# Cosine-similarity attention on one core: TensorE and ScalarE no longer wait on semaphores that they raise themselves

## Chip, core and metric

The kernel runs on one NeuronCore of a Trainium2 chip. The metric is device time in microseconds (us) for one execution; medians of several runs are given. "Slow" here means more than 1.5% above the fastest run of the same kernel. Ratios are the mean time of one kernel's fast runs over that of the other's of the same rounds, so they are not quite the ratio of the medians quoted beside them. "Span" is the time between the first and last instruction of the profiled execution; it is 1.7 to 2.0 us shorter than the device time. The experiments ran in three sets of rounds, on two chips; each set has its own runs of the kernel before (medians 240.59, 240.71 and 241.14 us), so kernels of different sets are best compared by their ratios.

## The reference

```python
def setup_inputs():
    batch, heads, seq, dim = 8, 12, 512, 64
    return {"Q": np.random.randn(batch, heads, seq, dim).astype(np.float32),   # K and V alike
            ..., "tau": 0.1}

def reference(Q, K, V, tau):
    Q_norm = Q / (np.linalg.norm(Q, axis=-1, keepdims=True) + 1e-10)
    K_norm = K / (np.linalg.norm(K, axis=-1, keepdims=True) + 1e-10)
    scores = np.einsum('bhqd,bhkd->bhqk', Q_norm, K_norm) / tau
    weights = np.exp(scores - np.max(scores, axis=-1, keepdims=True))
    weights = weights / (np.sum(weights, axis=-1, keepdims=True) + 1e-10)
    return np.einsum('bhqk,bhkd->bhqd', weights, V).astype(np.float32)
```

There are 96 heads. The kernel treats them as 48 pairs of heads.

## The kernel before

The kernel describes its work as a list of operations with an engine, a modelled cost and a list of the operations that each one needs. A small scheduler in the kernel puts the operations into one order per engine, and a writer then emits the instructions of each engine with semaphore waits. A semaphore is a counter: an operation can raise it when it has ended, and an engine can wait until it has reached a value. This is the writer's part that matters:

```python
    def run(self):
        nc = self.nc
        order = self.schedule()
        dma_sems, dma_count, last_out = {}, {}, {}
        for e, ops in order.items():
            for o in ops:
                for n in o.needs:
                    self.ops[n].used = True          # somebody waits for n: it must raise its semaphore
        # ... each used operation gets the next count of its engine's semaphore (o.sem, o.val)

        def write(engine, name):
            seen = {}
            for o in order[name]:
                want = {}
                for n in o.needs:
                    p = self.ops[n]
                    k = id(p.sem)
                    if p.val > max(seen.get(k, 0), want.get(k, (None, 0))[1]):
                        want[k] = (p.sem, p.val)
                for k, (sem, val) in want.items():
                    engine.wait_ge(sem, val)
                    seen[k] = val
                inst = o.emit(engine, o.bank) if o.bank else o.emit(engine)
                if o.sem is not None:
                    inst.then_inc(o.sem, o.inc)
```

For each pair `s`, TensorE does square sums (SSQ, 16 matmuls of 64 columns), transposes (TR, 8), scores (SCO, four chunks of two matmuls with 512 columns, one a head, each on half of the rows of the array) and the product of weights and V (PV, eight groups of four matmuls with 65 columns). ScalarE does one exp a chunk. VectorE divides by the row sums (RCP, NRM), and GpSimd (POOL in profiles) does most of the squaring before the square sums and part of the scaling. Matmuls write to PSUM, a memory in banks; the results of PV and of the square sums share two banks, and a bank comes free when VectorE has read it. Scores have two buffers, so the scores of chunk c need the exp of chunk c-2.

```python
            P.add(("SCO", s, c), "pe", 0.44, T0 + c - 3,
                  [("EVA", s), ("EXP", s, c - 2) if c >= 2 else key("EXP", s - 1, c + 2)], sco)
            P.add(("EXP", s, c), "act", 0.925, T0 + c,
                  [("SCO", s, c), key("PV", s - R_ET, 1, NT - 1)], lambda e, c=c, b=b: e.activation(...))
# ... [cut]
        for h in range(2):
            for t in range(NT):
                def pv(e, bank, h=h, t=t):
                    for c in range(NT):
                        last = e.matmul(
                            out=o_ps[bank][:, 65 * t : 65 * t + 65],
                            lhsT=et[iet][:, c, h, 128 * t : 128 * t + 128], rhs=vb[:, iq, c, h, :],
                            start=(c == 0), stop=(c == NT - 1))
                    return last

                op = P.add(("PV", s, h, t), "pe", 0.127, T0 + 4 + 2 * h + 0.4 * t,
                           [("EXP", s, NT - 1), ("VC", s)] + ([("PV", s, h, t - 1)] if t else []), pv,
                           take=("pv", s, h) if t == 0 else None)
# ... [cut: RCP needs the last of these groups]
            P.add(("NRM", s, h), "dve", 0.43, T0 + 5.6 + 2 * h, [("RCP", s, h), key("ST", s - R_O)],
                  lambda e, bank, h=h: e.tensor_tensor(out=ob[io][:, h], ...), give=("pv", s, h))
```

`("PV", s, h, t - 1)` is a need of one TensorE operation on another one. It keeps the four groups of a head in order for the scheduler, but the writer also turns it into a real wait.

## Time and profile before

| | before |
|---|---|
| device time, median of the first 3 runs | 241.84 us |
| span of the profiled run | 239.6 us |
| first exp starts, last exp ends, end of the span | 14.25, 232.8, 239.6 us |
| exps | 192, one every (232.8 - 14.25) / 192 = 1.138 us (the 1.133 of the prediction leaves out the length of the last exp) |

The page of the profile, part 1 (busy time of each engine, share of the span, instructions) and part 4 (the chain of work that ended last, by engine and by line):

```profile
PE 211.3 (88%) x3072; PEld 130.1 (54%) x3072; DVE 151.1 (63%) x481; ACT 192.6 (80%) x195; POOL 162.0 (68%) x148
...
PE 85%; issue 4%; ACT 3%; DVE 3%; DMA 2%; SPq 1%
PE ops L359 41%; PE scps L336 25%; PE ops L270 10%; PE tps L321 9%; ACT et L345 3%; DMA qk<-in_K_dram 2%; DVE qt L328 1%; SPq L252 1%; DVE sq L266 1%; DVE nps L288 0%; DVE nps L289 0%; DVE qn L315 0%; DVE ob L376 0%; DVE ys L293 0%; DVE nps L293 0%
```

TensorE (PE) is the chain: 85% of the span. "issue" is time in which an engine waited for nothing that the profile shows. TensorE's busy share alone would not say that it is the limit, because matmuls overlap: eight of about 197 ns take 0.42 us below. L359 is the PV matmul, L336 the scores, L345 the exp.

Part 5 of the page, three groups (line, engine, operation, output<-inputs, shapes, count | busy us, mean ns | idle time before, and what ended most of it):

```profile
L345 ACT ACTIVATE et<-scps 128x1024 bf16<-128x1024 f32 x192 | 189.2, 1023 | 32.7 <-PE scps L336 29.7
L359 PE MATMUL ops<-vb,et 128*128 128x65 bf16 x1536 | 108.3, 197 | 12.7 <-ACT et L345 1.1
...
L359 PEld LDWEIGHTS ops<-vb,et 128*128 128x128 bf16 x1536 | 67.1, 98 | 65.6 <-PE ops L359 47.8
```

ScalarE (ACT) stood idle for 29.7 us until scores came. The weight loads of PV (PEld) stood idle for 47.8 us until *other PV matmuls* ended; by an estimate from the idle times shown further below, about 34 us of this (191 x 0.18) stood directly behind a PV group.

What one such wait costs is seen in the chain of waits between 151.5 and 154.7 us (start, length, what, number of matmuls):

```profile
152.00 0.32 PE scps L336 x2
152.33 0.24 PE ops L359 x4
152.57 0.05 issue
152.62 0.31 PE ops L359 x4
152.93 0.05 issue
152.97 0.42 PE ops L359 x8
```

The group that starts at 152.62 waited for the group before it: 0.31 us, and 0.05 us until the next can start. The last line holds two groups, of which the second belongs to the next head and waits for no PV group: the two take 0.42 us, so the second adds only about 0.12 us.

The timeline of the weight loads shows the two kinds of idle time in front of PV (start, length, engine, line, operation, count, idle time before it):

```profile
147.70 0.17 PEld L359 LDWEIGHTS ops<-vb,et 128*128 128x128 bf16 x4 [0.23 <-PE tps L321]
148.06 0.17 PEld L359 LDWEIGHTS ops<-vb,et 128*128 128x128 bf16 x4 [0.18 <-PE ops L359]
148.41 0.30 PEld L359 LDWEIGHTS ops<-vb,et 128*128 128x128 bf16 x8 [0.18 <-PE ops L359]
...
150.58 0.23 PEld L321 LDWEIGHTS tps<-ident,qn 128*128 128x128 bf16 x4 [0.23 <-issue]
```

A group behind a PV group idles 0.18 us. A group behind scores idles 0.23 us, but so does a transpose behind scores (150.58), which waits for nothing on TensorE. A wait behind scores should therefore cost little.

### The profile page before, as it was taken

Reading aid. Unit: us, or ns where it says so; the run is one execution under the profiler, and the core shown is the slowest. Engines: PE = TensorE matmul, PEld = TensorE weight load, DVE = VectorE, ACT = ScalarE, POOL = GpSimd, SP = SyncE. Lnnn points to the kernel's source line nnn. Section 1 sums busy time; section 2 is a strip of 40 time slices with the busy share of each in tenths; the row PEclk is TensorE's granted clock in tenths of the full one; section 3 lists DMA queues with packets and bytes.
Section 4 is the critical chain, followed back from the end, with each engine's and each line's share of the span. In section 5 each row is a group of like instructions: output and inputs, shape, how many; then the busy total and the mean of one; then the engine's idle time right before and its main releaser. Section 6 shows DMA issues by size and latency. Waiting matters only on the chain.

```text
span 239.6 us, 7296 instructions
## 1 busy us (share of the span) xinstructions
PE 211.3 (88%) x3072; PEld 130.1 (54%) x3072; DVE 151.1 (63%) x481; ACT 192.6 (80%) x195; POOL 162.0 (68%) x148
## 2 busy tenths in 40 slices
PE   0489999889999999999999999999999999998773
PEld 0346556455655565565565565665665665654332
DVE  0667677465877767668657667667667767774322
ACT  3158998878798787898898898898898898887860
POOL 2399997929679868979939939949969935030000
PEclk9999999999999999999999999999999999999965
DMA  5999969695768569589695696699494412121121
GB/s 181 356 349 350 326 210 317 205 327 199 222 220 267 179 198 326 183 240 331 216 306 201 205 311 208 175 294 331 121 347 153 135 47 88 51 84 47 44 89 45
DMA packets 52256, 50.80 MB, mean 212 GB/s; under 512 B 3072, under 2 KB 52224, under 8 KB 52224
## 3 DMA queue, kind: packets, MB, share of 16 engines
q1 hardware_dynamic: 52224, 50.34, 65.6%
q8 instruction: 24, 0.39, 0.6%
q14 instruction: 8, 0.07, 0.1%
HBM read 37.75 MB, written 12.58 MB: 210 GB/s over the span
## 4 chain that ended last, share of the span: by engine, by line
PE 85%; issue 4%; ACT 3%; DVE 3%; DMA 2%; SPq 1%
PE ops L359 41%; PE scps L336 25%; PE ops L270 10%; PE tps L321 9%; ACT et L345 3%; DMA qk<-in_K_dram 2%; DVE qt L328 1%; SPq L252 1%; DVE sq L266 1%; DVE nps L288 0%; DVE nps L289 0%; DVE qn L315 0%; DVE ob L376 0%; DVE ys L293 0%; DVE nps L293 0%
## 5 line engine op out<-in xcount | busy, mean ns | idle before, releaser
L345 ACT ACTIVATE et<-scps 128x1024 bf16<-128x1024 f32 x192 | 189.2, 1023 | 32.7 <-PE scps L336 29.7
L359 PE MATMUL ops<-vb,et 128*128 128x65 bf16 x1536 | 108.3, 197 | 12.7 <-ACT et L345 1.1
L359 PEld LDWEIGHTS ops<-vb,et 128*128 128x128 bf16 x1536 | 67.1, 98 | 65.6 <-PE ops L359 47.8
L266 POOL TENSOR_TENSOR sq<-qk 128x1024 bf16<-128x1024 f32 x45 | 84.4, 1894 | 0.0
L315 POOL TENSOR_TENSOR qn<-qk,rk 128x512 bf16<-128x512 f32 x48 | 49.3, 1042 | 45.0 <-DVE rk L293 26.9
L336 PE MATMUL scps<-qt 64*128 64x512 bf16 x384 | 74.9, 392 | 3.0 <-ACT et L345 2.1
L373 DVE RECIPROCAL rd<-ops 128x4 f32<-128x4 f32 x96 | 17.3, 180 | 45.1 <-PE ops L359 44.8
L376 DVE TENSOR_TENSOR ob<-ops,rd 128x256 f32<-128x256 f32 x96 | 40.2, 422 | 2.6
L270 PE MATMUL ops<-sq,ident 128*128 128x64 bf16 x768 | 32.2, 197 | 8.9 <-ACT sq L263 6.4
L328 DVE COPY qt<-tps 128x1024 bf16<-128x1024 bf16 x48 | 33.0, 688 | 9.2 <-PE tps L321 8.6
L321 PE MATMUL tps<-ident,qn 128*128 128x128 bf16 x384 | 36.3, 224 | 0.5 <-DVE qt L328 0.5
L270 PEld LDWEIGHTS ops<-sq,ident 128*128 128x128 bf16 x768 | 27.7, 100 | 13.2 <-ACT sq L263 6.5
L351 POOL TENSOR_SCALAR vb<-vf 128x512 bf16<-128x512 f32 x48 | 29.6, 633 | 6.4 <-DMA vf<-in_V_dram 6.4
L315 DVE TENSOR_TENSOR qn<-qk,nps 128x512 bf16<-128x512 f32 x48 | 32.2, 670 | 0.0
L321 PEld LDWEIGHTS tps<-ident,qn 128*128 128x128 bf16 x384 | 22.9, 99 | 10.2 <-issue 5.6
L336 PEld LDWEIGHTS scps<-qt 64*128 64x128 bf16 x384 | 17.9, 93 | 17.1 <-ACT et L345 4.3
L280 DVE TENSOR_REDUCE nps<-ops 128x16 f32<-128x64 f32 x48 | 10.9, 227 | 17.2 <-PE ops L270 16.9
L288 DVE TENSOR_TENSOR nps<-nps,ys 128x32 f32<-128x32 f32 (+2 forms) x36 | 7.6, 210 | 1.2
L289 DVE SCALAR_TENSOR_TENSOR nps<-nps,ys 128x32 f32<-128x32 f32 (+2 forms) x36 | 7.5, 210 | 1.2
L263 ACT ACTIVATE sq<-qk 128x1024 bf16<-128x1024 f32 x2 | 2.1, 1056 | 6.7 <-DMA qk<-in_K_dram 6.7
L266 DVE TENSOR_TENSOR sq<-qk 128x1024 bf16<-128x1024 f32 x1 | 1.2, 1225 | 7.6 <-DMA qk<-in_K_dram 7.6
L297 DVE TENSOR_SCALAR ys<-nps 128x32 int32<-128x32 int32 (+2 forms) x18 | 3.6, 202 | 0.6
(11 smaller groups left out, 12.9 us busy)
## 6 DMA issues: line engine op xcount, KB each, us to landing
qk<-in_Q_dram SPq DMA_DIRECT2D x48, 256.0 KB, 4.5
qk<-in_K_dram SPq DMA_DIRECT2D x48, 256.0 KB, 5.4
vf<-in_V_dram SPq DMA_DIRECT2D x48, 256.0 KB, 4.7
out_dram<-ob SPq DMA_DIRECT2D x48, 256.0 KB, 4.5
```

What stands on the lines that cost most here:

```text
L266: lambda e: e.tensor_tensor(out=sqf, in0=data, in1=data, op=ALU.mult))
L270: last = e.matmul(out=o_ps[bank][:, 320:384], lhsT=ident[:, :], rhs=sq[iqs][:, :, 4 * k : 4 * k + 4], start=(k == 0), stop=(k == 15))
L280: lambda e, bank: e.tensor_reduce(out=x2[:, :, c8 : c8 + 8], in_=o_ps[bank][:, 320:384].rearrange("p (w g e) -> p w g e", w=2, e=4), axis= ...
L315: lambda e, w=w, r=r: e.tensor_tensor(out=qn[iqn][:, w].rearrange("p t h d -> p h t d"), in0=qk[iq][:, w].rearrange("p h (t d) -> p h t d" ...
L321: last = e.transpose(t_ps[:, w, t, :], qn[iqn][:, w, t].rearrange("p h d -> p (h d)"), ident[:, :])
L328: lambda e: e.tensor_copy(out=qt[iqt][:, :, :, :].rearrange("p w t x -> p (w t x)"), in_=t_ps[:, :, :, :].rearrange("p w t x -> p (w t x)")))
L336: last = e.matmul(out=sc_ps[:, 2 * b + h, :], lhsT=qt[iqt][64 * h : 64 * h + 64, 1, c, :], rhs=qt[iqt][64 * h : 64 * h + 64, 0, :, :], sta ...
L345: lambda e, c=c, b=b: e.activation(out=et[iet][:, c, :, :], in_=sc_ps[:, 2 * b : 2 * b + 2, :], func=ACT.Exp, scale=inv_tau))
L351: lambda e: e.tensor_scalar(out=vb[:, iq, :, :, 0:DIM].rearrange("p c h d -> p h c d"), in0=vf[iv][:, :, :].rearrange("p h (c d) -> p h c ...
L359: last = e.matmul(out=o_ps[bank][:, 65 * t : 65 * t + 65], lhsT=et[iet][:, c, h, 128 * t : 128 * t + 128], rhs=vb[:, iq, c, h, :], start=( ...
L373: lambda e, bank, h=h: e.reciprocal(out=rd[io][:, h, :], in_=grid(bank)[:, :, DIM]))
L376: lambda e, bank, h=h: e.tensor_tensor(out=ob[io][:, h], in0=grid(bank)[:, :, 0:DIM], in1=rd[io][:, h, :].unsqueeze(2).to_broadcast([128, ...
```

## The change

The intent is to take away waits of an in-order engine on its own semaphore. The scheduler still sees the needs; only the writer drops them, for TensorE ("pe") and ScalarE ("act").

```diff
@@ -110,8 +110,11 @@
         for e, ops in order.items():
             for o in ops:
-                for n in o.needs:
-                    self.ops[n].used = True
+                o.waits = [self.ops[n] for n in o.needs]
+                if e in ("pe", "act"):
+                    o.waits = [p for p in o.waits if p.eng != e]
+                for p in o.waits:
+                    p.used = True
@@ -131,8 +134,7 @@
             for o in order[name]:
                 want = {}
-                for n in o.needs:
-                    p = self.ops[n]
+                for p in o.waits:
                     k = id(p.sem)
```

The built programs differ only in this: 288 waits of TensorE on its own semaphore are gone (and the increments nobody reads any more). The order of instructions is the same on all five engines, and no ScalarE operation needs another one, so ScalarE's program does not change at all. Of the 288 waits, 191 stand directly behind another PV group and 97 behind other matmuls.

## The prediction

> **What bounds the kernel now.** TensorE. The chain of waits puts 85% of the span on TensorE matmuls, 41% on the P·V line alone, and about 96% in a steady stretch from 145.9 to 163.7 us (four pairs of heads, 4.44 us a pair). ScalarE is busy 192.6 us (80%), and the groups view puts 29.7 us of its idle time down to the score matmuls. Back-to-back exps follow each other every 0.924 us in the timeline (six in 5.64 us), so its 192 exps need at least 177 us.
>
> **What the change does.** It moves nothing: the order of instructions is the same on all five engines. It drops 288 waits, all on TensorE and all of one kind: the first matmul of a P·V group (4 matmuls, 65 columns) waiting for the last matmul of the previous group. ScalarE has no wait on itself, so nothing changes there. Correctness does not need these waits: the groups write different columns, and the Trainium skill (PSUM page "PSUM — Partial Sum Buffer", "Engine vs sequencer instructions") says matmuls start and complete in program order.
>
> **What one such wait costs.** In the chain of waits, a group that waits on its predecessor takes 0.30 us plus 0.05 us "issue"; a second group without the wait adds only 0.12 us (8 matmuls in 0.42 us). So 0.235 us each. The weight-load row shows the same: 0.18 us idle before the load. The skill ("TensorE: Matmul & The Clock Gate", "Step-by-step") says weight loads are pulled ahead of running matmuls; the wait forbids this between groups, and the trace agrees. Only 191 of the 288 waits follow directly on a P·V group. The other 97 follow score, transpose or square-sum matmuls; after scores, transposes without any wait on TensorE show the same 0.23 us of idle, so those waits are nearly free. Estimate: 191 x 0.235 = 45 us of TensorE time removed.
>
> **How much is on the path.** All of it until ScalarE takes over. In the steady stretch 14 waits fall in 17.77 us; without them TensorE needs 14.5 us (3.62 a pair), ScalarE 16 x 0.924 = 14.8 us (3.70 a pair). Only two score buffers couple the two, and TensorE's work between score pairs is uneven (0.55 to 1.14 us): counting the larger of it and 0.924 each time gives 15.8 us (0.987 an exp). GpSimd (3.56 us a pair) and VectorE (some 3.4 in the stretch with groups of two pairs) are close behind, so I expect 0.96 to 1.02 us an exp, against 1.133 now.
>
> Span: 14.25 us until the first exp (unchanged) + 192 x 0.98 = 188 + tail 5.4 us (6.8 less six waits of about 0.23 at the end, where the clock is low) = 207.8; plus 2.2 us between span and time: **210 us, 203 to 219**. Faster by over 2%: 0.97; within 2%: 0.025; slower: 0.005.
>
> **What would show it.** Weight loads' wait on P·V matmuls falls from 47.8 us to under 15. Sixteen P·V matmuls take about 0.6 us in the timeline, not 1.13. ScalarE's share goes from 80% to about 92%, its wait on scores from 29.7 us to under 15. The chain of waits has ScalarE as a large part (over 30%), TensorE well under 85%. First exp still at about 14.2 us. Score matmuls wait for ScalarE more than now (4.3 us). VectorE and GpSimd keep their busy times.
>
> **What would make it wrong.** GpSimd or VectorE becomes the limit in the first 100 us (GpSimd runs there without a break from 10.7 to 39.6 us): over 215. Groups after the change still do not overlap (a limit of weight load, not of the wait): 230 or more. ScalarE runs nearly without gaps: 201 to 203.

## The result, and the profile after

| | before | after |
|---|---|---|
| device time, median | 241.78 us (4 runs) | 206.24 us (4 runs: 205.14 to 207.87) |
| ratio of fast runs | 1 | 0.8537 (95%: 0.8461 to 0.8613) |
| span of the profiled run | 239.6 us | 205.6 us |
| until the first exp | 14.25 us | 14.16 us |
| first exp to end of the last | 218.6 us, 1.138 an exp | 186.8 us, 0.973 an exp |
| behind the last exp | 6.8 us | 4.6 us |

The span fell by 34.0 us: 0.1 at the head, 31.8 while exps run, 2.2 at the tail. The profiled run is one of the slower two of four (207.31 us). The mean clock granted to TensorE was 0.980 of full speed before and 0.984 after, so the clock explains little of the gain (only part of that at the tail, see below).

The same parts 1 and 4 of the page, after:

```profile
PE 182.0 (89%) x3072; PEld 120.3 (59%) x3072; DVE 146.6 (71%) x481; ACT 182.0 (89%) x195; POOL 161.8 (79%) x148
...
PE 56%; ACT 23%; DMA 11%; DVE 6%; SPq 1%; issue 1%; ACTq 0%; DVEq 0%
ACT et L347 22%; PE scps L338 20%; PE ops L361 18%; PE ops L272 10%; PE tps L323 8%; DMA out_dram<-ob 8%; DMA qk<-in_K_dram 3%; DVE qt L330 2%; DVE ob L378 2%; SPq L254 1%; ACT sq L265 1%; ACTq L151 0%; DVE nps L290 0%; DVE nps L282 0%; DVE rd L375 0%
```

And the same three groups of part 5, after:

```profile
L347 ACT ACTIVATE et<-scps 128x1024 bf16<-128x1024 f32 x192 | 178.6, 1058 | 11.5 <-PE scps L338 10.8
...
L361 PE MATMUL ops<-vb,et 128*128 128x65 bf16 x1536 | 75.0, 196 | 6.4 <-DVE ob L378 4.9
...
L361 PEld LDWEIGHTS ops<-vb,et 128*128 128x128 bf16 x1536 | 56.9, 98 | 36.7 <-issue 23.3
```

PV (now L361) fell from 41% of the chain to 18%, and from 108.3 to 75.0 us of busy time with the same 1536 matmuls of the same mean length (197 and 196 ns): they overlap now. No PV weight load waits for a PV matmul any more. The 23.3 us that are now called "issue" are the 0.23 us behind scores, which before were put down to the PV wait that ended at about the same time. The chain of waits after the change, between 135.6 and 137.5 us, reads:

```profile
135.68 0.32 PE scps L338 x2
136.00 0.66 PE ops L361 x16
136.66 0.32 PE scps L338 x2
136.99 0.48 PE ops L361 x12
```

Twelve matmuls behind scores take 0.48 us. Before, three such groups took 0.24 + 0.05 + 0.31 + 0.05 + 0.30 = 0.95 us (153.72 to 154.66 us). Two blocking waits cost 0.47 us, 0.235 each.

ScalarE's timeline after shows two regimes (idle time before each piece in brackets):

```profile
57.50 4.69 ACT L347 ACTIVATE et<-scps 128x1024 bf16<-128x1024 f32 x5 [0.68 <-PE scps L338]
64.40 15.24 ACT L347 ACTIVATE et<-scps 128x1024 bf16<-128x1024 f32 x16 [2.21 <-PE scps L338]
...
87.06 1.02 ACT L347 ACTIVATE et<-scps 128x1024 bf16<-128x1024 f32 x1 [1.69 <-PE scps L338]
88.59 1.02 ACT L347 ACTIVATE et<-scps 128x1024 bf16<-128x1024 f32 x1 [0.51 <-PE scps L338]
90.03 110.94 ACT L347 ACTIVATE et<-scps 128x1024 bf16<-128x1024 f32 x120 [0.41 <-PE scps L338]
```

From 90.03 us on, 120 exps run in 110.94 us, 0.924 each: the spacing that unhindered exps had before the change (six in 5.64 us). ScalarE is then the limit. Earlier there are gaps that the old kernel did not have in this form. The two largest after the first exp (2.21 us before 64.40 and 1.69 us before 87.06) come from VectorE, which waits for an output store. The first of them is shown here (first its line in the timeline of VectorE, then the chain of waits over the same stretch, both after the change):

```profile
63.25 0.42 DVE L378 TENSOR_TENSOR ob<-ops,rd 128x256 f32<-128x256 f32 x1 [2.80 <-DMA out_dram<-ob]
```

```profile
56.41 0.47 DVE qt L330
56.88 0.00 issue
56.88 6.28 DMA out_dram<-ob
...
63.25 0.44 DVE ob L378
63.69 0.05 issue
63.74 0.30 PE ops L361 x4
64.03 0.34 PE scps L338 x2
64.38 0.02 issue
64.40 1.94 ACT et L347 x2
```

A store issued at 56.88 us lands 6.28 us later. The normalization that wants its buffer waits for it, PV waits for the PSUM bank that the normalization holds, the scores queue behind PV, and ScalarE runs dry. This wait is new: before, no VectorE instruction waited for a store.

### The profile page after: what moved, and what is told of

It reads as the page before. It is cut to its first block, busy times and chain, and to the rows that moved or that the text cites. A ratio compares the mean times of both kernels' runs of the same rounds, so it can differ in the third digit from the quotient of the medians.

```text
span 205.6 us, 7296 instructions
## 1 busy us (share of the span) xinstructions
PE 182.0 (89%) x3072; PEld 120.3 (59%) x3072; DVE 146.6 (71%) x481; ACT 182.0 (89%) x195; POOL 161.8 (79%) x148
## 4 chain that ended last, share of the span: by engine, by line
PE 56%; ACT 23%; DMA 11%; DVE 6%; SPq 1%; issue 1%; ACTq 0%; DVEq 0%
ACT et L347 22%; PE scps L338 20%; PE ops L361 18%; PE ops L272 10%; PE tps L323 8%; DMA out_dram<-ob 8%; DMA qk<-in_K_dram 3%; DVE qt L330 2%; DVE ob L378 2%; SPq L254 1%; ACT sq L265 1%; ACTq L151 0%; DVE nps L290 0%; DVE nps L282 0%; DVE rd L375 0%
## 5 line engine op out<-in xcount | busy, mean ns | idle before, releaser
L347 ACT ACTIVATE et<-scps 128x1024 bf16<-128x1024 f32 x192 | 178.6, 1058 | 11.5 <-PE scps L338 10.8
L361 PE MATMUL ops<-vb,et 128*128 128x65 bf16 x1536 | 75.0, 196 | 6.4 <-DVE ob L378 4.9
L338 PE MATMUL scps<-qt 64*128 64x512 bf16 x384 | 75.8, 394 | 4.5 <-ACT et L347 2.8
L361 PEld LDWEIGHTS ops<-vb,et 128*128 128x128 bf16 x1536 | 56.9, 98 | 36.7 <-issue 23.3
L338 PEld LDWEIGHTS scps<-qt 64*128 64x128 bf16 x384 | 18.4, 93 | 21.6 <-ACT et L347 5.0
```

Source lines behind the costliest of these rows:

```text
L338: last = e.matmul(out=sc_ps[:, 2 * b + h, :], lhsT=qt[iqt][64 * h : 64 * h + 64, 1, c, :], rhs=qt[iqt][64 * h : 64 * h + 64, 0, :, :], sta ...
L347: lambda e, c=c, b=b: e.activation(out=et[iet][:, c, :, :], in_=sc_ps[:, 2 * b : 2 * b + 2, :], func=ACT.Exp, scale=inv_tau))
L361: last = e.matmul(out=o_ps[bank][:, 65 * t : 65 * t + 65], lhsT=et[iet][:, c, h, 128 * t : 128 * t + 128], rhs=vb[:, iq, c, h, :], start=( ...
```

## The experiments

The theory (A): a wait on TensorE's own semaphore costs the rest of the round trip of the matmul that it names, about 0.235 us where that is the matmul just issued, and nothing where it is old. TensorE was the limit, so the time fell by nearly all of it until ScalarE took over. Rivals: it is the increments (B), each wait costs the same (C), or the wait instruction has a fixed handling cost (D). All experiments leave the order of instructions on every engine as it was; only the last two pairs of kernels leave instructions out or add some.

### Increments kept, waits gone

```diff
-                for p in o.waits:
-                    p.used = True
+                for n in o.needs:
+                    self.ops[n].used = True
```

Expected: 

> The changed kernel, but every P.V group still raises the TensorE semaphore (288 increments that nobody reads). Theory A, the waits cost: 206 us, as the changed kernel. Rival B, the increments cost and the waits are free: near 241 us. If increments carry a part, between 209 and 235 us.

Measured: 206.56 us (before, in the same rounds: 240.59), ratio 0.8575, correct. Rival B falls: 288 increments that nobody waits for cost nothing that shows.

### Only the 97 waits behind other matmuls kept, and only the 191 behind PV kept

```diff
+            prev = None
             for o in ops:
                 o.waits = [self.ops[n] for n in o.needs]
-                if e in ("pe", "act"):
+                if e == "pe" and not (prev is not None and prev.key[0] != "PV"):   # == "PV" in the mirror image
                     o.waits = [p for p in o.waits if p.eng != e]
+                prev = o
```

Expected of the 97: 

> Only the 97 waits stay whose group does not follow directly on another P.V group (it follows scores, transposes or square sums). Theory A (a wait costs only what is left of the predecessor's completion when TensorE gets to it): 206 to 208 us, as the changed kernel. Rival C (every wait on the own semaphore costs the same, 35.6 us / 288 = 0.124 us each): 206 + 97 x 0.124 = 218 us.

Expected of the 191: 

> The mirror image: the 191 waits that follow directly on a P.V group stay, the other 97 go. Theory A: 240 to 242 us, as the kernel before. Rival C (all waits equal): 241.8 - 97 x 0.124 = 230 us.

Measured: 206.47 us with the 97 waits (ratio 0.8582) and 240.94 us with the 191 (ratio 1.0009). All of the gain hangs on the 191 waits that follow directly on a PV group. Rival C falls.

### The wait moved to an older group

```diff
+        groups = []
         for e, ops in order.items():
             for o in ops:
                 o.waits = [self.ops[n] for n in o.needs]
-                if e in ("pe", "act"):
+                if e == "pe":
+                    mine = any(p.eng == e for p in o.waits)
                     o.waits = [p for p in o.waits if p.eng != e]
+                    if o.key[0] == "PV":
+                        groups.append(o)
+                        if mine and len(groups) > 2:          # 8 in the second kernel
+                            o.waits.append(groups[-1 - 2])
```

Expected of two back: 

> As many waits as before on TensorE's own semaphore (285 of 288), but each waits for the P.V group two before it instead of the one before it. Theory A (what costs is the round trip of the group just issued, 0.355 us, against 0.12 us of work a group): in a run of four groups only one of three waits still blocks, for 0.355 - 0.24 = 0.115 us, so some 7 us of TensorE time come back in place of 45, and much of that hides: 206 to 211 us. Rival D (a wait on the own semaphore costs some 0.2 us of handling whatever it waits for): near 241 us.

Expected of eight back: 

> As many waits as before on TensorE's own semaphore, each for the P.V group eight before it, which has always long ended. Theory A: as the changed kernel, 206 us. Rival D (the wait instruction itself costs): 218 to 241 us.

Measured: 207.61 us two back (before 240.59; ratio 0.8601; one of four runs, 209.89, counted as slow and is not in the ratio) and 205.99 us eight back (before 240.71; ratio 0.8535; one run, 208.04, counted as slow). The built kernels have 287 and 282 waits on the own semaphore (the 285 of the expectation was a slip). So 282 such waits are free when they name a group that has ended. Rival D falls. The chain of waits of the kernel with two back shows the dose:

```profile
133.16 0.32 PE scps L344 x2
133.48 0.71 PE ops L367 x16
134.19 0.32 PE scps L344 x2
134.51 0.58 PE ops L367 x12
```

Sixteen matmuls behind scores take 0.71 us instead of 0.59 to 0.66, twelve 0.58 instead of 0.48. The expected remainder was 0.355 - 0.24 = 0.115 us for one blocking wait.

### Half of the waits gone

```diff
-                if e in ("pe", "act"):
+                if e == "pe" and o.key[0] == "PV" and o.key[2] == 0:     # the first head of each pair only
```

Expected: 

> The waits of the first head of each pair go (144, of which 84 follow directly on a P.V group), those of the second stay (144, 107 direct). Theory A, TensorE stays the limit all through at this dose: 241.8 - 84 x 0.235 = 222 us. A rival in which ScalarE or the store waits already limit after half: 210 to 216 us. A rival in which the second half of the waits is what counts (nothing until all are gone): above 232 us.

Measured: 221.04 us (before 240.71; ratio 0.9185). That is 19.7 us for 84 direct waits, 0.234 us each. At this dose every removed wait counts in full, so TensorE was the limit throughout. All 191 at this price are 45 us; the whole change brought 35.5. The second half of the waits is worth less because another limit comes in between.

### Eight output buffers, after and before

```diff
     R_QK, R_V, R_SQ, R_QN, R_QT, R_ET, R_O, R_X = 18, 6, 6, 3, 3, 3, 4, 3
+    R_OB = 8
-    ob = [sb(f"ob{i}", [128, 2, NT, DIM], f32) for i in range(R_O)]
+    ob = [sb(f"ob{i}", [128, 2, NT, DIM], f32) for i in range(R_OB)]
         # ob[io] and the store's semaphore become those of s % R_OB; and, after scheduling:
+        for o in self.list:
+            if o.key[0] == "NRM":
+                late = ("ST", o.key[1] - 8)
+                o.needs = [n for n in o.needs if n[0] != "ST"] + ([late] if late in self.ops else [])
```

Expected of the changed kernel with eight: 

> The changed kernel with eight output buffers instead of four, the order of instructions on every engine unchanged; only the normalization's wait for the store of four pairs earlier moves to the store of eight pairs earlier. Theory E (the ScalarE gaps at 57 to 65 and 79 to 90 us come from normalization waiting for a store): VectorE's wait on stores falls from 6.2 us to 0, ScalarE's wait on scores from 10.8 us to about 5, time 198 to 202 us. Rival F (another limit stands right behind, GpSimd or transfers): the waits on stores go, ScalarE's wait on scores stays at 9 us or more, time 204 to 207 us.

Expected of the kernel before with eight: 

> The kernel before, all 288 waits in place, with the same eight output buffers. Theory E says no store held it up at its slower pace, so 241 to 242 us, unchanged. If output buffers were a limit of their own: 236 us or less.

Measured: 201.10 us (200.89 to 201.60) with the change, ratio 0.8359; 241.09 us without it, ratio 1.0024. ScalarE's timeline of the faster one:

```profile
56.49 19.84 ACT L352 ACTIVATE et<-scps 128x1024 bf16<-128x1024 f32 x21 [0.68 <-PE scps L343]
76.83 2.85 ACT L352 ACTIVATE et<-scps 128x1024 bf16<-128x1024 f32 x3 [0.50 <-PE scps L343]
80.12 114.32 ACT L352 ACTIVATE et<-scps 128x1024 bf16<-128x1024 f32 x124 [0.44 <-PE scps L343]
```

VectorE no longer waits for a store, and ScalarE's wait for scores fell from 10.8 to 6.2 us, of which 3.38 are in front of the first exp. The same buffers do nothing for the slower kernel. So stores were a limit that the change itself brought to light, worth 4 to 5 us (5.1 between the medians, 4.3 by the ratios 0.8537 and 0.8359). Runs also agree better: 0.7 us apart in place of 2.7. This version beats both kernels.

### TensorE work taken away (a wrong result)

```diff
-            for k in range(16):
+            for k in range(0, 16, 2):
                 last = e.matmul(
                     out=o_ps[bank][:, 320:384], lhsT=ident[:, :], rhs=sq[iqs][:, :, 4 * k : 4 * k + 4],
-                    start=(k == 0), stop=(k == 15))
+                    start=(k == 0), stop=(k == 14))
```

Expected of the kernel before: 

> The kernel before with half of the square-sum matmuls left out (8 of 16 a pair; a wrong result on purpose), nothing else changed. A matmul there takes 0.47 us / 16 = 0.029 us, so 48 x 8 x 0.029 = 11 us of TensorE work go. Theory A, TensorE limits the kernel before: 241 - 11 = 230 us (228 to 233).

Expected of the changed kernel with eight output buffers: 

> The same cut of 11 us of TensorE work in the changed kernel with eight output buffers (201.1 us). Theory G, ScalarE is the limit there: 199 to 201 us. Rival H, TensorE is still the limit or shares it (its share busy is 91%): 197 us or less, 190 if all of it counts.

Measured: 233.48 us against 241.14 (ratio 0.9694), and 198.39 us against the 201.10 of the earlier rounds (ratio to before 0.8232). Both miss the stated ranges a little, and in ways that qualify the theory. The kernel before gained 7.7 us and not 11: TensorE is its limit, but not every matmul's time counts in full. The trace shows where part of the other 3 us went: over 16 exps of the steady stretch (17.77 us before, 17.22 us here) the square sums' part of the chain of waits falls from 1.90 to 0.71 us, but 0.63 us of VectorE's reciprocal and normalization enters it, for which a PV group now waits. The fast version gained 2.7 us (3.1 by the ratios), which lies between the two theories. The last 124 exps took 113.77 us in place of 114.32, so there TensorE's work hardly matters; most of the rest came before 80 us. This fits ScalarE as the limit of the later part, and TensorE sharing it in the first 80 us.

### ScalarE work added

```diff
+            def exp(e, c=c, b=b):
+                if c == NT - 1:
+                    e.activation(out=scratch[s % 4][:, :], in_=sc_ps[:, 2 * b, :], func=ACT.Exp, scale=inv_tau)
+                return e.activation(...)        # as before
```

Expected of the kernel before: 

> The kernel before with one more exp of 512 columns a pair into a scratch tile (right result). By half of the 0.924 us of 1024 columns it costs ScalarE at least 0.46 us, 48 x 0.46 = 22 us in all. Theory A: ScalarE has 4.44 - 3.70 = 0.74 us to spare a pair, so most of it hides: 241 to 249 us. If ScalarE were a limit before: 260 us or more.

Expected of the changed kernel with eight output buffers: 

> The same extra exp in the changed kernel with eight output buffers. Theory G, ScalarE is the limit: 201 + 22 = 223 us or a little more (221 to 229). Rival H: below 215 us.

Measured: 247.63 us against 241.14 (ratio 1.0280), and 222.90 us against 201.10 (ratio to before 0.9229). The same extra work of 48 x 0.46 = 22 us costs 6.5 us where TensorE is the limit and 21.8 us (21.0 by the ratios) where ScalarE is. This is the clearest sign that the limit has moved.

## Why the prediction was right

The predicted time was 210 us with a range of 203 to 219; measured were 206.2.

- **What is removed.** 288 waits, 191 of them direct, 0.235 us each: held. Half the dose gave 0.234 us for each direct wait, the 97 others were free, and no wait behind an old group cost anything.
- **Correctness.** The Trainium skill ("PSUM — Partial Sum Buffer", "Engine vs sequencer instructions") says matmuls start and complete in program order. The changed kernel gave the right result, as did every variant without these waits. A group's four matmuls also write only their own 65 columns of the bank. With matmuls in order, the wait guarded nothing.
- **The mechanism.** The skill ("TensorE: Matmul & The Clock Gate", "Step-by-step: what each phase is for") says that the loads of the next weights are pulled ahead of matmuls in flight. The traces agree: with the wait a group's first load sits idle for 0.18 us behind the group before it, without it the loads and matmuls of 12 stream through in 0.48 us.
- **The sum.** Head: 14.25 predicted, 14.16 measured. Exps: 0.98 us each predicted, 0.973 measured (0.960 in the profiled run with the 97 waits, 0.972 in that with eight back). Tail: 5.4 us predicted, 4.6 measured. Between span and time: 2.2 predicted, 1.7 measured. Before, TensorE ran most of the tail at half its clock (0.50 from 230 to 236 us) and the last groups took 0.46 us each; after, the 32 matmuls behind the last exp, busy for 3.38 us before, take 1.15 us at full clock. The prediction had priced the tail at the low clock, so this part of the gain was not foreseen.
- **ScalarE takes over.** Shown by the 120 exps at 0.924 us, and, in the version with eight output buffers, by the extra exp that costs nearly all of its 22 us. The share of 92% came out as 89%, and ScalarE's part of the chain of waits as 23%, below the "over 30%" that was asked for: three output stores (8% of the chain) stand in part of its place.
- **A right number with a partly wrong reason.** The prediction allowed 0.98 us an exp in place of 0.924, naming GpSimd and VectorE as close behind and the uneven work between score pairs. From the uneven work it had worked out 0.987 us for a steady stretch late in the kernel; there the exps ran at 0.924, so the unevenness cost nothing that shows. What was lost was lost before 90 us, and the prediction did not name output stores. That this loss came out at nearly the size of the wrong term was luck. Eight output buffers brought the exps to (194.44 - 13.15) / 192 = 0.944 us, so 0.02 to 0.03 us above ScalarE's own pace were waits for stores (0.960 to 0.973 with four buffers). The rest lies before 80 us; cutting TensorE's work took away some of it. What GpSimd and VectorE contribute was not separated.
- **What the title says of ScalarE** is empty in this kernel: it never waits for itself.

Two things stay open. Of the 3 us that the kernel before did not give back for shorter square sums, only part was traced. And the same trick on VectorE could not be tried: its operations read what the one just before wrote.

## What to carry to other kernels

On TensorE, a wait on its own semaphore blocks until the named matmul has come all the way back; behind a short group that tripled the group's time here (0.355 against 0.12 us), while a wait on something old was free, so look at how far back a wait reaches and not at how many waits there are. When the limiting engine gets faster, recount every ring of buffers at the new pace: the four output buffers were ample at 4.4 us a pair and cost 4 to 5 us after the change (3.7 us a pair where ScalarE is the limit). To find which engine limits, add a known amount of work to one engine and see how much of it comes back: 6.5 of 22 us before, 21.8 of 22 in the changed kernel with eight output buffers.

## What the Trainium skill lacked or had wrong

- No page gives the cost of a TensorE wait on its own semaphore. Here it was 0.235 us of added time when the matmul named was just issued, about 0.11 us when it was two groups back, and none when it was eight groups back ("TensorE: Matmul & The Clock Gate" would be the place).
- "TensorEngine Tiling (Array Packing)", "Key Properties", says that changing the tiling mode drains TensorE, without a number. Here weight loads for the full array idled 0.23 us behind scores that use half of the rows each, with and without a semaphore wait (101 such waits, 23.3 us, after the change). That this is the drain is an inference from the page; it may as well be the time that the score matmuls of 512 columns (0.39 us a pair) still need, and no run here tells the two apart.
- "TensorE: Matmul & The Clock Gate", "Why this matters for your kernels", advises against idle gaps above about 3 us. That row says nothing of shorter gaps. Here a gap of 1.77 us (84.3 to 86.1 us, the wait for a store) was followed by half the clock from about 86.4 to 89.8 us, and score pairs of 0.61 in place of 0.39 us, while a gap of 2.36 us before 63.7 us was not. The trace shows a difference between the two: the clock changed at 86.36, 89.77 and 202.41 us, one and 33 steps of 3.41 us apart, and on this grid the gap of 1.77 us lies within one step, while that of 2.36 us is split in two (at 62.47 us). The kernel with waits eight back shows the same: a gap of 2.39 us within a step (82.87 to 85.26 us) was followed by half the clock from 85.35 to 88.76 us, one of 1.92 us that is split (60.39 to 62.31 us) was not. How much idle time within a step it takes was not measured.
- "ScalarE: Activation LUTs", "What ACT_TABLE_LOAD costs", gives an activation 186 ns + 0.833 ns an element and an overlap of 93 ns with the next one: by an estimate from these figures, 1024 elements take 1.039 us and follow each other every 0.946 us. Here an exp was 1.023 us long where it did not have to queue, and 0.924 us apart: 2% quicker, which over 192 exps is 4 us. The exps read PSUM; the two squares of 1024 elements that read the other on-chip memory, SBUF, took 1.056 us. The page does not say which memory its figure is for, so it may be a difference of place and not an error.
